# Decay weights of a recurrent layer: their tanh with tokens on the partitions, their running sums as matrix products

## The chip, the cores and the metric

The kernel runs on one core of a Trainium2 chip. The metric is device time in microseconds (us), the median of several runs. The engines are TensorE (PE; its weight loads are PEld), VectorE (DVE), ScalarE (ACT), GpSimd (POOL) and SyncE (SP), which here only issues transfers between SBUF and DRAM.

## The reference, cut to what matters

The program is a step through four layers: a long convolution (hyena), an attention layer, a recurrent layer (RWKV-7) and again hyena. Only the third, the recurrent one, is touched. It has D = 1024 channels in 16 heads of 64, T = 1152 tokens (1024 + 128), two directions n, and a state S for each head:

```python
r, k, v, z = einsum('pbld,pde->pble', [xr, xk, xv, xg], w_in)
wl = w0[n] + tanh(xw @ w1[n]) @ w2[n]                 # rank 64
decay = exp(-exp(-softplus(-wl) - 0.5))
a  = sigmoid(a0[n] + (xa @ a1[n]) @ a2[n])            # rank 64
kk = heads(k * k_k);  kk = kk * rsqrt(sum(kk * kk, -1) + 1e-12)
kd = heads(k * (1 + (a - 1) * k_a));  bd = kk * heads(a)
# at each token, forwards for n = 0 and backwards for n = 1:
S = S * decay + (S @ -kk) bd^T + v kd^T;   y = S @ r
```

Since exp(-softplus(-x)) is the sigmoid of x, the logarithm of a decay is -exp(-0.5) (1 + tanh(wl / 2)) / 2. The kernel takes the tokens in chunks of 64 and needs, in each chunk, the products of the decays up to every token, and their inverses. These are exponentials of running sums of 1 + tanh(wl / 2).

## The kernel before

Constants: P = 128 partitions, KC = 8 blocks of 128 channels (index b), NG = 3 groups of GRP = 384 tokens (index g), 6 chunks of 64 in a group. Activations lie with channels on the partitions and tokens along the row.

The recurrent layer (`rwkv`, line 1569) has three stages. First `dense` (line 1696) runs a list of jobs, each a projection of one block of 128 output channels: for each g it accumulates 8 x 3 fp32r matmuls of 384 columns (`mm3`, lines 262 to 264: high part times high part, and two products with low parts) in one PSUM bank, and an `evac` function takes the bank out. The order of jobs is r (8 jobs), `wjob` (the rank-64 hidden part of the decays, 3 steps for both directions), v (8), `ajob` (the same for a), k (8), z (8). The weights of the next job are loaded after a job's first step into tiles with tags `wh` and `wl`, two of each. The inputs of a job are mixed from the activations by `mix` (line 1648) into four slots, as far ahead as slots come free (`mix_ahead`); it works in tiles with tags `mix` and `nb`, two of each.

The second stage overlaps with the k and z jobs: `weave` (line 1888) takes in turns the 44 last steps of `dense` and the generators `rows_of(b)` (line 1802), three pieces for each g, 24 groups in all. A group loads r, v and k (`rvk`, line 1812, in a tile with tag `mix`), makes the decays' pre-activation from the hidden part with `lora2` (lines 1740 to 1745: one matmul with 128 rows and one with 64), takes tanh on ScalarE (L1822), adds 1 (L1824), forms the running sums of a chunk with a scan on VectorE, one for each direction (L1827; `rst` resets it every 65 columns), turns the second direction's sums round on GpSimd (L1846, L1847) and takes exponentials (L1840 to L1849). W holds the decay products and `ei` their inverses, all in SBUF. The norms of the keys are spread by transposes (L1832) into PSUM, and L1835 makes the normalised keys `kk` in SBUF. From these, a and k come the rows `ct` and `bk` (L1855 to L1865), which are stored for the third stage, and a bonus term (L1862 to L1871, with one plain fp32 matmul, L1869, that becomes two instructions). The third stage, the chunked recurrence, only reads what is stored.

PSUM has eight banks; `set_banks` (line 1874) lets tags mm, tp and ax take all eight in turn through the first two stages. Each bank is one tile, so a tile that takes a bank waits for its last reader. The instructions of an engine run in the order in which the planner put them at build time, which follows the order of the program except where it finds other work ready earlier; on the chip that order is fixed.

Of the kernel before, what the change touches and what calls it, by code (L numbers as in the profile page):

```python
# [132 lines left out]
def rwkv_constants():  # L133
    q = np.arange(64)
    blk = np.kron(np.eye(2), np.ones((64, 64)))
    eye = np.zeros((P, P))
    eye[:, :64] = np.concatenate([np.eye(64)] * 2)
    eye[:, 64:66] = np.kron(np.eye(2), np.ones((64, 1)))
    row, colm = q[:, None], q[None, :]
    mask = np.zeros((P, 2, P))  # L140
    for n, (st, inc) in enumerate(((row < colm, row <= colm), (row > colm, row >= colm))):
        mask[:, n, :64] = np.concatenate([st] * 2)
        mask[:, n, 64:] = np.concatenate([inc] * 2)
    lm = np.zeros((P, 4, 2, 64))
# [15 lines left out]
    reset = (np.arange(6 * 65) % 65 != 0).astype(np.float32)  # L160
    return (np.stack([blk, eye], 1).astype(np.float32), mask.astype(np.float32), four.astype(np.float32),
            levels.reshape(P, 4, 256).astype(np.float32), reset)


def weave(*jobs):

    for _ in woven(*jobs):
        pass
# [29 lines left out]
def chain_gens(*gens):  # L198
    for g in gens:
        yield from g  # L200
# [22 lines left out]
class Prog:  # L223
# [1345 lines left out]
    def rwkv(self, i, rest):  # L1569
# [20 lines left out]
        v_.tensor_scalar(hka[:, :, 1], vec[:, :, 5], -0.5, 1.0, op0=M, op1=Ad)  # L1590
        v_.tensor_scalar(hka[:, :, 2:], vec[:, :, :4], 0.5, None, op0=M)
        wcs = keep.tile([P, KC, 2 * NCH], F32, name="wcs")
        cdec = math.exp(-0.5)
        eps = keep.tile([P, 2], F32, name="eps")
        v_.memset(eps[:, 0:1], 1e-12)
# [100 lines left out]
        def dense(jobs):  # L1696

            nxt, later = self.load_w(jobs[0][0]), None  # L1700
            for n, (_, mi, evac) in enumerate(jobs):
                wh, wl = nxt
                for g in range(NG):
                    o = self.psum("mm")[:, :GRP]
                    hh, hl = slot(3 * mi + g)
                    for k in range(KC):
                        self.mm3(o, wh[:, k], wl[:, k], hh[:, k], hl[:, k], k == 0, k == KC - 1)
                    if later:
                        later()
                    later = evac(g, o)  # L1710
                    if g == 0 and n + 1 < len(jobs):
                        nxt = self.load_w(jobs[n + 1][0])
# [5 lines left out]

        def lora(mi, name, fn):

            hid = [pool.tile([P, T], F32R, name=f"{name}{n}") for n in range(2)]
# [24 lines left out]

        wjob, whid = lora(1, "w", AF.Tanh)
        ajob, ahid = lora(3, "a", AF.Copy)

        def project(p, mi, evac):  # L1750
            return [(A["rw_w_in"][p, :, b * P:(b + 1) * P], mi, lambda g, ps, b=b: evac(b, g, ps)) for b in range(KC)]
# [50 lines left out]
        def rows_of(b):  # L1802

            if b in (0, 1, 2, 4):
                bs = slice(b, b + max(b, 1))
                s_.activation(norms[:, bs], norms[:, bs], AF.Sqrt, bias=eps[:, 0:1])
                v_.reciprocal(norms[:, bs], norms[:, bs])
            w2 = [lora2_weights(name, b) for name in "wa"]
            for g in range(NG):
                gs = grp[g]  # L1810
                x = pool.tile([P, 3, GRP], F32, tag="mix", name="rvk", bufs=2)
                nc.sync.dma_start(x, rvk[b, :, :, gs])
                r, v, k = (x[:, y] for y in range(3))
# [4 lines left out]
                W = pool.tile([P, 2, 6, 65], F32, tag="nb", name="W", bufs=2)  # L1818
                v_.memset(W[:, :, :, 0], 0.0)
                c3 = lambda x: x.rearrange("p (c t) -> p c t", t=64)  # L1820
                for n in range(2):
                    s_.activation(W[:, n, :, 1:], c3(lora2(w2[0], whid, g, n)), AF.Tanh, scale=0.5,  # L1822
                                  bias=hka[:, b, 2 + n:3 + n])
# [4 lines left out]
                rx = self.mp.tile([P, 512], F32, tag="mprod", name="rx", bufs=1)[:, :GRP].rearrange("p (c t) -> p c t", t=64)  # L1828
                s_.copy(rx, norms[:, b, 6 * g:6 * g + 6].unsqueeze(2).broadcast_to([P, 6, 64]))
                pb = self.psum("tp")[:, :GRP]  # L1830
                for o in range(3):
                    nc.tensor.transpose(pb[:, o * P:(o + 1) * P], rx[:, 2 * o:2 * o + 2].rearrange("p a b -> p (a b)"),  # L1832
                                        self.ident)
                kk = row2()
                v_.scalar_tensor_tensor(kk, k, vec[:, b, 4:5], pb, op0=M, op1=M)  # L1835
                for n in range(2):
                    s_.activation(an[:, n], c3(lora2(w2[1], ahid, g, n)), AF.Tanh, scale=0.5,
                                  bias=hka[:, b, 4 + n:5 + n])
                yield
                s_.activation(wcs[:, b].rearrange("p (d c) -> p d c", d=2)[:, :, 6 * g:6 * g + 6], W[:, :, :, 64], AF.Exp,  # L1840
                              scale=-cdec / 2)
                ei = [self.mp.tile([P, 512], F32, tag=f"macc{n}", name="ei", bufs=1)[:, :6 * 65] for n in range(2)]
                ei = [x.rearrange("p (c t) -> p c t", t=65) for x in ei]
                s_.activation(ei[0], W[:, 0], AF.Exp, scale=cdec / 2)
                last = ei[1][:, :, 64:65]
                g_.tensor_copy(last, W[:, 1, :, 64:65])  # L1846
                g_.tensor_tensor(W[:, 1], last.broadcast_to([P, 6, 65]), W[:, 1], Su)  # L1847
                s_.activation(ei[1], W[:, 1], AF.Exp, scale=cdec / 2)
                s_.activation(W, W, AF.Exp, scale=-cdec / 2)  # L1849
# [3 lines left out]
                upto, before = (AP(W.tensor, W.offset + x, [W.ap[0], [390 + 1 - 2 * x, 2], [65, 6], [1, 64]]) for x in (1, 0))  # L1853
                ei = [ei[0][:, :, 1:], ei[1][:, :, :64]]
                g_.tensor_tensor(kd, kd, both(k), M)  # L1855
                v_.tensor_tensor(ct[:, :, :, 0], before, both(kk), M)
# [23 lines left out]
        weave((part_gen(run, 6 * KC + 6 - DS), 6 * KC + 6 - DS), (rest, 44))  # L1880
        mtmp.close()
        pool2 = tmp.enter_context(tc.tile_pool(name="rw2", bufs=1, side="right", reuse_waits="tile"))
        rst = pool2.tile([P, 6 * 65], F32, name="rst")
        nc.sync.dma_start(rst, A["rw_reset"].partition_broadcast(P))
# [395 lines left out]
def host_arrays(x):  # L2280
# [37 lines left out]
    r["rw_const"], r["rw_mask"], r["rw_lmask"], r["rw_levels"], r["rw_reset"] = rwkv_constants()  # L2318
    return r


# [17 lines left out]
```

## Time and profile before

| | us |
|---|---|
| median of three runs | 4572.27 (4570.69 to 4586.91) |
| the profiled execution's own time | 4590.18 |
| its span | 4588.4 |
| projections of r, v, from | 2030 to 2331 |
| `ajob` and first k steps | 2331 to 2382 |
| row groups beside k and z jobs | 2382 to 2791 |

Over the span TensorE is busy for 89%, VectorE for 76%, ScalarE for 52% and GpSimd for 51%. The stretch of the change is under a tenth of the span, so shares of the whole say little of it; the rows below are from that stretch. Busy time of TensorE counts the whole passage of a matmul, and neighbours overlap, so the distance between two starts, not the length of one, tells what a stream of matmuls costs.

### The profile page before, as it was taken

The page shows a single profiled execution, that of the slowest core. Times are in us where ns is not written, and L with a number is a line of the kernel's source. Part 1 is how long each engine was busy: PE and PEld are TensorE (multiplying, and loading weights), DVE is VectorE, ACT ScalarE, POOL GpSimd, SP SyncE. Part 2 cuts the span into 40 slices and gives each one's busy share as a digit, 9 for nine tenths or more (in the row PEclk, how much of TensorE's full clock was granted, in tenths as well). Part 3 has the DMA queues.
Part 4 walks back from the last instruction along what each step waited for, and adds up shares of the span by engine and source line. Part 5 has one row for each costly group of instructions (what it writes and reads, how often), then busy time and mean ns, then how long its engine had stood idle before and what let it go on. Part 6 is the DMA issues. An engine that isn't in the chain of part 4 may idle for free. (4 is left out here: it accounts for less than half of the span.)

```text
span 4588.4 us, 83899 instructions
## 1 busy us (share of the span) xinstructions
PE 4061.0 (89%) x30888; PEld 3510.6 (77%) x30888; DVE 3504.3 (76%) x6147; ACT 2392.5 (52%) x5468; POOL 2360.3 (51%) x1902
## 2 busy tenths in 40 slices
PE   7988988889999999879979786999999889988988
PEld 4888888678777776658867575878888678878986
DVE  7777888655998999687587997677767668967877
ACT  5554433455666666453455553666666456543331
POOL 3655766253677877455555564333333233466550
PEclk8999999999999999989988797999999899999999
DMA  5755555643000000326635464222322424665455
GB/s 169 239 181 176 164 156 157 191 149 99 19 22 21 18 28 30 121 91 203 188 108 198 145 222 136 59 79 84 83 75 68 142 93 120 214 205 153 141 155 179
DMA packets 490982, 583.04 MB, mean 127 GB/s; under 512 B 59818, under 2 KB 378332, under 8 KB 489932
## 3 DMA queue, kind: packets, MB, share of 16 engines
q1 hardware_dynamic: 489068, 576.70, 40.7%
q8 instruction: 244, 4.00, 0.4%
q14 instruction: 166, 1.36, 0.1%
q10 hardware_dynamic: 1504, 0.98, 0.1%
HBM read 413.74 MB, written 161.37 MB: 125 GB/s over the span
## 5 line engine op out<-in xcount | busy, mean ns | idle before, releaser
L262 PE MATMUL ps_mm<-hh,wh 128*128 128x384 f32 x1728 | 597.0, 347 | 47.4 <-ACT hh L267 24.0
L263 PE MATMUL ps_mm<-hl,wh 128*128 128x384 f32 x1728 | 595.6, 345 | 2.8 <-DVE hl L268 1.8
L264 PE MATMUL ps_mm<-hh,wl 128*128 128x384 f32 x1728 | 594.5, 344 | 2.7 <-POOL wl L268 2.7
L1499 POOL TENSOR_TENSOR sm<-sm,pf 128x512 f32<-128x512 f32 x288 | 443.4, 1540 | 121.8 <-ACT pf L1492 48.8
L268 POOL TENSOR_TENSOR wl<-wraw,wh 128x512 fp32r<-128x512 f32 x212 | 331.5, 1581 | 187.4 <-ACT wh L267 175.3
L262 PEld LDWEIGHTS ps_mm<-hh,wh 128*128 128x128 f32 x1728 | 335.9, 195 | 55.5 <-ACT hh L267 25.1
L1497 DVE TENSOR_TENSOR wl<-pf,wh 128x512 fp32r<-128x512 f32 x288 | 352.8, 1235 | 6.6 <-ACT wh L1493 5.8
L263 PEld LDWEIGHTS ps_mm<-hl,wh 128*128 128x128 f32 x1728 | 336.2, 195 | 7.5 <-DVE hl L268 4.4
L264 PEld LDWEIGHTS ps_mm<-hh,wl 128*128 128x128 f32 x1728 | 336.0, 194 | 6.4 <-POOL wl L268 3.8
L305 POOL TENSOR_TENSOR macc<-macc,mprod 128x512 f32<-128x512 f32 x140 | 211.8, 1513 | 178.0 <-ACT mprod L304 155.4
L263 PE MATMUL ps_mm<-mx,wh 128*128 128x384 f32 x680 | 253.6, 373 | 37.9 <-DVE mx L1669 36.9
L262 PE MATMUL ps_mm<-mx,wh 128*128 128x384 f32 x680 | 255.9, 378 | 19.9 <-ACT mx L1668 6.1
L262 PE MATMUL ps_mm<-woh,hh 128*128 128x512 f32 x576 | 233.8, 407 | 37.0 <-ACT hh L267 34.6
L2144 POOL TENSOR_TENSOR tot<-SV,wcs 64x128 f32<-64x128 f32 x288 | 115.6, 405 | 267.9 <-DVE SV L2172 245.2
L264 PE MATMUL ps_mm<-mx,wl 128*128 128x384 f32 x680 | 247.0, 364 | 3.1 <-POOL wl L268 3.1
L1492 ACT ACTIVATE pf<-ps_st 128x512 f32<-128x512 f32 x288 | 172.3, 598 | 144.9 <-POOL sm L1499 53.3
L264 PE MATMUL ps_mm<-woh,hl 128*128 128x512 f32 x576 | 234.1, 406 | 3.7 <-DVE hl L268 3.7
L302 DVE SCALAR_TENSOR_TENSOR macc<-modw,cond,macc 128x512 f32<-128x512 f32 x140 | 156.5, 1118 | 103.3 <-DMA modw<-mod_w 102.4
L1437 DVE TENSOR_REDUCE mx<-ps_pj 128x1 f32<-128x512 f32 (+2 forms) x400 | 220.4, 575 | 17.2 <-PE ps_pj L1436 16.4
L263 PE MATMUL ps_mm<-wol,hh 128*128 128x512 f32 x576 | 231.8, 402 | 0.0
L304 ACT ACTIVATE mprod<-modw,cond 128x512 f32<-128x512 f32 x140 | 101.3, 723 | 205.5 <-POOL macc L305 108.6
L1493 ACT ACTIVATE wh<-ps_st 128x512 fp32r<-128x512 f32 x336 | 194.3, 578 | 0.0
(560 smaller groups left out, 13149.2 us busy)
## 6 DMA issues: line engine op xcount, KB each, us to landing
cst<-cst SPq DMA_DIRECT2D x175, 384.0 KB
modw<-mod_w SPq DMA_DIRECT2D x160, 256.0 KB
wraw<-hy_w_in SPq DMA_DIRECT2D x128, 256.0 KB
kd<-kt SPq DMA_DIRECT2D x72, 384.0 KB
kt<-kd SPq DMA_DIRECT2D x72, 384.0 KB
cst<-cst SPq DMA_DIRECT2D x41, 512.0 KB
ctd<-ct SPq DMA_DIRECT2D x24, 768.0 KB
bkd<-bk SPq DMA_DIRECT2D x24, 768.0 KB
```

The source lines that it names most:

```text
L262: mm(ps, lh, rh, start=start, stop=False)
L263: mm(ps, lh, rl, start=False, stop=False)
L264: mm(ps, ll, rh, start=False, stop=stop)
L268: (lo_eng or self.nc.gpsimd).tensor_tensor(lo, src, hi, ALU.subtract)
L302: nc.vector.scalar_tensor_tensor(acc[0], w, s, acc[0], op0=ALU.mult, op1=ALU.add)
L305: nc.gpsimd.tensor_tensor(acc[1], acc[1], wp, ALU.add)
L1437: nc.vector.tensor_reduce(mx[:, t, j:j + 1], ps, AX.X, ALU.max)
L1492: nc.scalar.activation(pf, s, AF.Exp, scale=scale)
L1493: nc.scalar.activation(ph, s, AF.Exp, scale=scale)
L1497: nc.vector.tensor_tensor(pl, pf, ph, ALU.subtract)
L1499: nc.gpsimd.tensor_tensor(sm, sm, pf, ALU.add)
L2144: g_.tensor_tensor(tot[h], SV[e][h, jsl], wc[h].unsqueeze(2).broadcast_to([64, 2, 64]), M)
```

## The change

The tanh of the decays is taken before the row groups, with tokens on the partitions, in two new jobs between v and `ajob`. Each (one for a direction) makes, for every tile of 128 tokens, two blocks of 512 channels: three matmuls (hidden part times high part of w2, 64 rows of it times the low part, and a product with constant rows of ones that adds the bias w0), a tanh from PSUM, and a store of the 128 x 1024 tile to a DRAM array `thd`. In the row groups the running sums are matrix products of these tiles with triangular 0/1 matrices `tri` (a sum is over the tokens, which now are the contraction); the +1 of each token enters as a one-row product with a table of counts. The second direction's triangle sums backwards, so its turning round is gone. The two sums of a group stay in PSUM (three banks of their own); W is their exponential in SBUF, the inverse decays are written over the sums in PSUM, and `kk` stays in the bank of the transposes. The other tags share five banks from there on. The hidden part of the decays moves to a pool that is closed before the row groups.

```diff
+        ones_r = keep.tile([P, 2, P], F32R, name="ones_r")
...
+            load = lambda n: self.load_w(jobs[n][0]) if jobs[n][1] is not None else jobs[n][0]()
+            nxt, later = load(0), None
             for n, (_, mi, evac) in enumerate(jobs):
                 wh, wl = nxt
+                if mi is None:
+                    nxt = load(n + 1)
+                    if later:
+                        later = later()
+                    yield from evac(wh, wl)
+                    continue
...
+        def decays(n):
+            h = half[n]
+
+            def steps(wh, wl):
+                for t in range(NT):
+                    ts = slice(t * P, (t + 1) * P)
+                    x = pool.tile([P, 3, GRP], F32, tag="mix", name="th", bufs=2).rearrange("p a c -> p (a c)")[:, :D]
+                    for cs in (slice(0, 512), slice(512, D)):
+                        ps = self.psum("ax")
+                        nc.tensor.matmul(ps, whid[n][:, ts], wh[:, cs], start=True, stop=False)
+                        nc.tensor.matmul(ps, whid[n][h, ts], wl[h, cs], start=False, stop=False)
+                        nc.tensor.matmul(ps, ones_r[:, n], wl[:, cs], start=False, stop=True)
+                        s_.activation(x[:, cs], ps, AF.Tanh, scale=0.5)
+                    nc.sync.dma_start(thd[:, t, :, n].rearrange("b p c -> p b c"), x.rearrange("p (b c) -> p b c", c=P))
...
-        jobs = project(0, 0, evac_r) + [wjob] + project(2, 2, evac_v) + [ajob]
+        jobs = project(0, 0, evac_r) + [wjob] + project(2, 2, evac_v) + [decays(0), decays(1), ajob]
...
-            w2 = [lora2_weights(name, b) for name in "wa"]
+            w2 = lora2_weights("a", b)
             for g in range(NG):
                 gs = grp[g]
+                th = pool2.tile([P, 3, 2, P], F32, tag="th", name="th", bufs=2)
+                nc.sync.dma_start(th, thd[b, 3 * g:3 * g + 3].rearrange("o p n c -> p o n c"))
...
+                sums = [self.psum("w")[:, :6 * 65] for _ in range(2)]
+                for n, ps in enumerate(sums):
+                    for o in range(3):
+                        own = ps[:, o * 130:(o + 1) * 130]
+                        nc.tensor.matmul(own, ones_r[:1, 1], cnt[:, n], start=True,
+                                         stop=False)
+                        nc.tensor.matmul(own, th[:, o, n], tri[:, n], start=False, stop=True)
...
-                kk = row2()
-                v_.scalar_tensor_tensor(kk, k, vec[:, b, 4:5], pb, op0=M, op1=M)
+                v_.scalar_tensor_tensor(kk, k, vec[:, b, 4:5], kk, op0=M, op1=M)
...
-                v_.tensor_scalar(W[:, :, :, 1:], W[:, :, :, 1:], 1.0, None, op0=Ad)
-                for n in range(2):
-                    w1 = W[:, n].rearrange("p c t -> p (c t)")
-                    v_.tensor_tensor_scan(out=w1, data0=rst, data1=w1, initial=0.0, op0=M, op1=Ad)
...
+                W = pool.tile([P, 2, 6, 65], F32, tag="nb", name="W", bufs=2)
+                for n, ps in enumerate(sums):
+                    s_.activation(W[:, n].rearrange("p c t -> p (c t)"), ps, AF.Exp, scale=-cdec / 2)
+                    s_.activation(ps, ps, AF.Exp, scale=cdec / 2)
...
+        self.set_banks(mm_tp_ax=(0, 1, 2, 3, 4), w=(5, 6, 7))
         weave((run, 6 * KC - 4), (chain_gens(*(rows_of(b) for b in range(KC))), 9 * KC))
```

## Rows read from the trace of the kernel before

**Rows 1.** Busy time by stretch: engines with record counts, granted clock, DMA share.

```profile
core 0: us, PE busy (x) PEld busy (x) DVE busy (x) ACT busy (x) POOL busy (x), PEclk, DMA share, GB/s
2331.00:2382.00 51.00, 35.65 (x143) 30.10 (x142) 39.76 (x78) 31.40 (x57) 21.88 (x13) 0.73 0.22 62
...
2560.00:2660.00 100.00, 72.59 (x282) 56.99 (x280) 89.70 (x118) 53.34 (x102) 60.97 (x42) 0.78 0.49 164
2660.00:2760.00 100.00, 87.65 (x406) 73.26 (x405) 93.49 (x100) 53.24 (x108) 63.56 (x47) 0.93 0.64 213
...
2382.00:2791.00 409.00, 337.17 (x1500) 279.37 (x1502) 350.18 (x426) 216.13 (x413) 243.88 (x175) 0.83 0.56 187
```

**Rows 2.** TensorE in order of time (start, length in us) in the row groups.

```profile
2564.56 0.81 PEld L1785 LDWEIGHTS ps_tp<-rwc,po 128*128 128x128 f32 x6
...
2705.43 0.42 PE L1743 MATMUL ps_ax<-w,w 128*128 128x384 f32 x1
2705.78 0.43 PE L1744 MATMUL ps_ax<-w,w 64*128 64x384 f32 x1
2706.14 0.44 PE L1743 MATMUL ps_ax<-w,w 128*128 128x384 f32 x1
...
2724.40 0.49 PE L1832 MATMUL ps_tp<-ident,rx 128*128 128x128 f32 x3
...
2728.65 0.34 PE L262 MATMUL ps_mm<-mx,wh 128*128 128x384 f32 x1
...
2729.17 0.34 PE L262 MATMUL ps_mm<-mx,wh 128*128 128x384 f32 x1
...
2751.15 0.81 PE L1869 MATMUL ps_ax<-row,rwc 128*128 128x384 f32 x2
```

**Rows 3.** Busy time of L262 alone, then of L1743 alone, by stretch.

```profile
2660.00:2760.00 100.00, 39.12 (x104) 21.36 (x104) 0.93 0.64 213
2660.00:2760.00 100.00, 10.84 (x29) 5.10 (x29) 0.93 0.64 213
```

**Rows 4.** Groups by line, 2382 to 2791: busy us, mean ns | idle before.

```profile
L1827 DVE TENSOR_TENSOR_SCAN W<-rst,W 128x390 f32<-128x390 f32 x48 | 63.6, 1361 | 0.5
L1864 DVE SCALAR_TENSOR_TENSOR bk<-bk,ei 128x384 f32<-128x384 f32 x48 | 57.6, 1219 | 2.4 <-ACT ei L1848 1.5
L1865 DVE TENSOR_TENSOR bk<-bk,ei 128x384 f32<-128x384 f32 x48 | 40.5, 882 | 2.6 <-POOL row L1862 2.4
L1856 DVE TENSOR_TENSOR ct<-W,row 128x768 f32<-128x768 f32 x24 | 37.2, 1549 | 2.8 <-POOL w L268 2.3 <-ACT W L1849 0.4
L1860 DVE SCALAR_TENSOR_TENSOR bk<-bk,row 128x768 f32<-128x768 f32 x24 | 31.0, 1291 | 3.3 <-ACT bk L1850 3.0
L1822 ACT ACTIVATE W<-ps_ax,hka 128x384 f32<-128x384 f32 x48 | 26.1, 579 | 12.9 <-PE ps_ax L1744 8.9 <-DVE ct L1856 3.4 <-POOL ei L1846 0.4
L1847 POOL TENSOR_TENSOR W<-ei,W 128x390 f32<-128x390 f32 x24 | 25.8, 1074 | 1.3 <-ACT wcs L1840 0.2
L1824 DVE TENSOR_SCALAR W<-W 128x768 f32<-128x768 f32 x24 | 19.8, 826 | 13.4 <-ACT W L1822 13.2
```

**Rows 5.** One line's instructions: duration ns min/median/max, first and last start.

```profile
L1864 DVE SCALAR_TENSOR_TENSOR bk<-bk,ei x48: 527/1274/2202, 2391.5 to 2785.5; 128x384 f32<-128x384 f32 x48
L1835 DVE SCALAR_TENSOR_TENSOR row<-rvk,rvec,ps_tp x24: 593/605/616, 2382.9 to 2780.1; 128x384 f32<-128x384 f32 x24
L1870 DVE TENSOR_TENSOR row<-ps_ax,rvk x24: 526/550/558, 2406.1 to 2790.1; 128x384 f32<-128x384 f32 x24
```

**Rows 6.** The chain that ended last, 2367 to 2791: start us, us, what.

```profile
2768.22 2.41 DVE bk L1864 x2
...
2771.50 1.76 DVE W L1827 x2
...
2774.87 5.10 DMA rvk<-rvk
...
2790.73 3.81 DMA bvd<-row
```

**Rows 7.** Waits of TensorE, 2300 to 2384: us in total, times, longest.

```profile
PE ps_mm L263 <- DVE mx L1669: 11.3, 7, 2.8
```

**Rows 8.** Waits of TensorE, 2382 to 2791: us in total, times, longest.

```profile
PE ps_ax L1869 <- DVE row L1867: 22.8, 10, 6.5
```

More of the change, by code (lines that the diff above doesn't have):

```diff
@@ L159, in rwkv_constants @@
     four = np.stack([four, four * (1 - 2 * lm_eye)], 1)
-    reset = (np.arange(6 * 65) % 65 != 0).astype(np.float32)
+    t65, two = np.arange(65), np.arange(P)
+    tri = np.zeros((P, 2, 2, 65))
+    for c in range(2):
+        own, s = (two // 64 == c)[:, None], (two % 64)[:, None]
+        tri[:, 0, c] = own & (s < t65)
+        tri[:, 1, c] = own & (s >= t65)
+    counts = np.stack([np.tile(t65, 2), np.tile(64 - t65, 2)]).reshape(1, -1)
     return (np.stack([blk, eye], 1).astype(np.float32), mask.astype(np.float32), four.astype(np.float32),
-            levels.reshape(P, 4, 256).astype(np.float32), reset)
+            levels.reshape(P, 4, 256).astype(np.float32), tri.reshape(P, 2, 130).astype(np.float32),
+            counts.astype(np.float32))
 def weave(*jobs):
@@ L1592, in rwkv @@
         wcs = keep.tile([P, KC, 2 * NCH], F32, name="wcs")
+        thd = self.dp.tile([KC, NT, P, 2, P], F32, name="thd")
+        ones_r = keep.tile([P, 2, P], F32R, name="ones_r")
+        for n, h in enumerate(half):
+            s_.activation(ones_r[h, n], self.ones[h], AF.Copy, scale=0.0)
+            s_.copy(ones_r[half[1 - n], n], self.ones[half[1 - n]])
         cdec = math.exp(-0.5)
@@ L1696, in dense @@
         def dense(jobs):
-            nxt, later = self.load_w(jobs[0][0]), None
+            load = lambda n: self.load_w(jobs[n][0]) if jobs[n][1] is not None else jobs[n][0]()
+            nxt, later = load(0), None
             for n, (_, mi, evac) in enumerate(jobs):
                 wh, wl = nxt
+                if mi is None:
[4 more added lines that the diff above has]
+                    continue
                 for g in range(NG):
@@ L1711, in dense @@
                     if g == 0 and n + 1 < len(jobs):
-                        nxt = self.load_w(jobs[n + 1][0])
+                        nxt = load(n + 1)
                     if n + 1 == len(jobs) or jobs[n + 1][1] != mi:
@@ L1719, in lora @@
         def lora(mi, name, fn):
-            hid = [pool.tile([P, T], F32R, name=f"{name}{n}") for n in range(2)]
+            hid = [(mpool if name == "w" else pool).tile([P, T], F32R, name=f"{name}{n}") for n in range(2)]
             def evac(g, ps):
@@ L1748, in rwkv, with decay_weights @@
         ajob, ahid = lora(3, "a", AF.Copy)
+        def decay_weights(n):
+            h, o = half[n], half[1 - n]
+            wh, wl = (self.wp.tile([P, KC, P], F32R, tag=x, name=x).rearrange("p k c -> p (k c)") for x in ("wh", "wl"))
+            for cs in (slice(0, 512), slice(512, D)):
+                raw, rows = (self.wp.tile([P, 4, P], F32, tag="wraw", name=x).rearrange("p k c -> p (k c)")
+                             for x in ("w2r", "w2b"))
+                for x in half:
+                    nc.sync.dma_start(raw[x], A["rw_w2"][h, cs])
+                s_.copy(wh[:, cs], raw)
+                g_.tensor_tensor(wl[h, cs], raw[h], wh[h, cs], Su)
+                v_.memset(rows[o], 0.0)
+                for x in (o.start, o.start + 32):
+                    nc.sync.dma_start(rows[x:x + 1], A["rw_wb"][n:n + 1, cs])
+                s_.copy(wl[o, cs], rows[o])
+                x = slice(o.start + 32, o.stop)
+                v_.tensor_tensor(wl[x, cs], rows[x], wl[x, cs], Su)
+            return wh, wl
+        def decays(n):
[4 more added lines that the diff above has]
+                    x = pool.tile([P, 3, GRP], F32, tag="mix", name="th", bufs=2).rearrange("p a c -> p (a c)")[:, :D]
+                    for cs in (slice(0, 512), slice(512, D)):
+                        ps = self.psum("ax")
[4 more added lines that the diff above has]
+                    nc.sync.dma_start(thd[:, t, :, n].rearrange("b p c -> p b c"), x.rearrange("p (b c) -> p b c", c=P))
+                    if t % 3 == 2:
+                        yield
+            return lambda: decay_weights(n), None, steps
         def project(p, mi, evac):
@@ L1815, in rows_of @@
                 an, kd = bk[:, :, :, 0], bk[:, :, :, 1]
-                W = pool.tile([P, 2, 6, 65], F32, tag="nb", name="W", bufs=2)
-                v_.memset(W[:, :, :, 0], 0.0)
+                sums = [self.psum("w")[:, :6 * 65] for _ in range(2)]
[5 more added lines that the diff above has]
+                        nc.tensor.matmul(own, th[:, o, n], tri[:, n], start=False, stop=True)
@@ new lines, in rows_of @@
+                rx = self.mp.tile([P, 512], F32, tag="mprod", name="rx", bufs=1)[:, :GRP].rearrange("p (c t) -> p c t", t=64)
+                s_.copy(rx, norms[:, b, 6 * g:6 * g + 6].unsqueeze(2).broadcast_to([P, 6, 64]))
+                kk = self.psum("tp")[:, :GRP]
+                for o in range(3):
+                    nc.tensor.transpose(kk[:, o * P:(o + 1) * P], rx[:, 2 * o:2 * o + 2].rearrange("p a b -> p (a b)"),
+                                        self.ident)
+                v_.scalar_tensor_tensor(kk, k, vec[:, b, 4:5], kk, op0=M, op1=M)
@@ L1828, in rows_of @@
[L1828 to L1833, printed above, removed]
-                kk = row2()
@@ L1835, in rows_of @@
-                v_.scalar_tensor_tensor(kk, k, vec[:, b, 4:5], pb, op0=M, op1=M)
-                for n in range(2):
-                    s_.activation(an[:, n], c3(lora2(w2[1], ahid, g, n)), AF.Tanh, scale=0.5,
-                                  bias=hka[:, b, 4 + n:5 + n])
-                yield
-                s_.activation(wcs[:, b].rearrange("p (d c) -> p d c", d=2)[:, :, 6 * g:6 * g + 6], W[:, :, :, 64], AF.Exp,
-                              scale=-cdec / 2)
-                ei = [self.mp.tile([P, 512], F32, tag=f"macc{n}", name="ei", bufs=1)[:, :6 * 65] for n in range(2)]
@@ L1843, in rows_of @@
[L1843 to L1849, printed above, removed]
+                    s_.activation(an[:, n], c3(lora2(w2, ahid, g, n)), AF.Tanh, scale=0.5, bias=hka[:, b, 4 + n:5 + n])
@@ new lines, in rows_of @@
+                yield
+                W = pool.tile([P, 2, 6, 65], F32, tag="nb", name="W", bufs=2)
+                for n, ps in enumerate(sums):
+                    s_.activation(W[:, n].rearrange("p c t -> p (c t)"), ps, AF.Exp, scale=-cdec / 2)
+                    s_.activation(ps, ps, AF.Exp, scale=cdec / 2)
+                s_.copy(wcs[:, b].rearrange("p (d c) -> p d c", d=2)[:, :, 6 * g:6 * g + 6],
+                        AP(W.tensor, W.offset + 64, [W.ap[0], [390 - 64, 2], [65, 6]]))
@@ L1853, in rows_of @@
                 upto, before = (AP(W.tensor, W.offset + x, [W.ap[0], [390 + 1 - 2 * x, 2], [65, 6], [1, 64]]) for x in (1, 0))
+                ei = [x.rearrange("p (c t) -> p c t", t=65) for x in sums]
                 ei = [ei[0][:, :, 1:], ei[1][:, :, :64]]
@@ L1879, in rwkv @@
         mix_ahead(-1)
-        weave((part_gen(run, 6 * KC + 6 - DS), 6 * KC + 6 - DS), (rest, 44))
+        weave((part_gen(run, 6 * KC + 12 - DS), 6 * KC + 12 - DS), (rest, 44))
         mtmp.close()
         pool2 = tmp.enter_context(tc.tile_pool(name="rw2", bufs=1, side="right", reuse_waits="tile"))
-        rst = pool2.tile([P, 6 * 65], F32, name="rst")
-        nc.sync.dma_start(rst, A["rw_reset"].partition_broadcast(P))
+        tri = pool2.tile([P, 2, 130], F32, name="tri")
+        nc.sync.dma_start(tri, A["rw_tri"])
+        cnt = pool2.tile([1, 2, 130], F32R, name="cnt")
+        raw = self.mp.tile([P, 512], F32, tag="macc0", name="cnr", bufs=1)[:1, :260]
+        nc.sync.dma_start(raw, A["rw_counts"])
+        s_.copy(cnt.rearrange("p n c -> p (n c)"), raw)
         row2 = lambda: self.mp.tile([P, 512], F32, tag="modw", name="row", bufs=2)[:, :GRP]
@@ L2317, in host_arrays @@
     r["state"] = f(x["state_rwkv"][0, 0].transpose(0, 1, 3, 2))
-    r["rw_const"], r["rw_mask"], r["rw_lmask"], r["rw_levels"], r["rw_reset"] = rwkv_constants()
+    r["rw_const"], r["rw_mask"], r["rw_lmask"], r["rw_levels"], r["rw_tri"], r["rw_counts"] = rwkv_constants()
+    r["rw_wb"] = f(x["rw_w0"][0])
     return r
```

2 lines of the change are left out of this document (removed).

## The prediction

> **What bounds the kernel now.** I first looked for the stage that holds the edited lines, with the view of busy time by stretch of time [rows 1]. The stage in which the row groups are made (line 1802) runs from 2382 to 2791 us, 409 us with 24 groups, so 17.0 us a group. VectorE is busy for 350.2 us of it, TensorE for 337.2, and the granted TensorE clock averages 0.83. Read alone, this says that VectorE ends last. But a busy TensorE isn't yet a TensorE at its peak, so I counted what it has to issue. When it streams, matmuls of 384 columns start 0.17 us apart [rows 2]: three steps from 2728.65 to 2729.17, so 0.173 each. A step of `dense` is 8 x 3 = 24 of them, 4.15 us. The product of `lora2` is a pair, one matmul with 128 rows and one with 64: alternating, they start 0.35 and 0.36 us apart [rows 2], so a change between 128 and 64 rows costs about 0.19 us beside the 0.173, and a pair takes 0.73. L1869 is 0.81 for its two, the three transposes of L1832 0.49, six matmuls of L1785 0.81 (from the weight loads).
>
> The stage's issue time is then 44 steps x 4.15 = 183; 24 groups x 4 pairs x 0.73 = 70; 24 x 0.81 = 19; 24 x 0.49 = 12; 22 x 0.81 = 18; together 302 us, 74% of 409. By stretch it is less even. From 2660 to 2760 there are 104 records of each dense line and 29 of L1743 [rows 3]: 3 x 104 x 0.173 = 54, 29 x 0.73 = 21, and 6 groups of L1869 and L1832 at 1.3 = 8, so 83 of 100 us at a granted clock of 0.93. TensorE has little room there. From 2560 to 2660, where the last input mixes also load VectorE, TensorE records fall to 282 and the clock to 0.78 [rows 1]: there VectorE really ends last. So a change that moves work from VectorE to TensorE meets two limits that lie close together.
>
> **Part 1: what leaves VectorE.** Gone are the scans L1827 (48 x 1.361 = 63.6 us) and the +1 of L1824 (24 x 0.826 = 19.8) [rows 4], 83 us. A second saving is less visible. L1864, all of whose tensors lie in SBUF, takes 527 ns at least but 1274 at the median and 2202 at most, while L1835 and L1870, which read one operand from PSUM, stay within 593 to 616 and 526 to 558 [rows 5]. GpSimd works beside all three. With inverse decays and keys in PSUM, L1864 should fall from 1219 to about 605, L1865 from 882 to 550, L1856 and L1860 from 1549 and 1291 [rows 4] to about 1000 (an estimate: their 768 elements against L1870's 384, twice 0.55 less one start): 48 x 0.61 + 48 x 0.33 + 24 x 0.55 + 24 x 0.29 = 29 + 16 + 13 + 7 = 65 us. VectorE goes from 350 to about 202 us, half of the stage. If it gained nothing from PSUM it would still be 267, 65%, so it no longer ends last by itself. GpSimd loses L1847 (25.8 us) and the small copy before it, and ScalarE's tanh of L1822 moves to an earlier stage. Both engines were idle for 40% or more [rows 1], so I cost that at nothing.
>
> **Part 2: what comes to TensorE in the same stage.** The decays' `lora2` pairs go: 48 x 0.73 = 35 us. In their place each group gets 6 sums of 130 columns: one one-row product that adds the counts (`cnt`), and one plain fp32 product `th` x `tri`, which like L1869 becomes two instructions. No row of this stage shows a one-row matmul between 128-row ones. The nearest is the 128/64 alternation, 0.19 a change, and a sum has two changes. The weights of plain fp32 matmuls follow each other in 0.81 / 6 = 0.135 us [rows 2], more than 130 columns need (2 x 130 / 384 x 0.173 = 0.12). So a sum costs 2 x 0.19 + 0.07 + 0.27 = 0.72 us, and 144 of them 104 us. If the change of rows were free: 0.34 each, 49 us. If each change cost 0.25, as under a stall, 0.84, 121 us. I take 104, since the alternation is the same kind of step in the same stage.
>
> A rule bears on exactly this gap. The Trainium skill (TensorEngine Tiling (Array Packing), Key Properties) says that changing the tiling mode, not only the tile, drains the engine. No run here shows it for one row; by it the sum is the 104 us, and without it 49.
>
> So TensorE's issue time goes from 302 to 302 - 35 + 104 = 371 us. With VectorE out of the way I let it fill 0.88 of the stage: more than the 0.83 of its best stretch here, less than 1, because the groups still hand work around four engines. 371 / 0.88 = 422 us, 13 us more than now. Bounds: free changes give (302 - 35 + 49) / 0.88 = 359 (50 less); a fill of only 0.83 gives 447 (38 more). At the end of the stage the last group's chain loses its two scans (1.76) and about half of the 2.41 us of its L1864 [rows 6]: 3 us less.
>
> **Part 3: the new job in the projection stage.** `decays` makes 36 blocks of 512 columns, three matmuls each. By columns one is 512 / 384 x 0.173 = 0.23; the middle one uses 64 rows, so two changes: 3 x 0.23 + 2 x 0.19 = 1.07, 39 us in all. But each 128-token tile (two blocks, 2.1 us) is stored to DRAM, 512 KB, from a tile with tag `mix`, of which there are two. A store of 192 KB takes 3.81 us to land and a load of 576 KB takes 5.10 [rows 6]. I take 4.5, and 1.2 us for two tanh (L1822 takes 0.58 for 384 columns [rows 4]). Two tiles in flight then give (1.2 + 4.5) / 2 = 2.85 us a tile, 18 x 2.85 = 51 us. ScalarE needs 21 us of that and VectorE nearly nothing. The weights of `decays` are loaded under the last v job. What is queued behind: the job after it, `ajob`, needs a weight tile with tag `wh`, and both are held by the two `decays` jobs, so `ajob` can start only when the first is done.
>
> Some of it is covered. From 2331 to 2382 TensorE shows 143 records, about 25 us of work in 51 us at a clock of 0.73 [rows 1], and it waits 11.3 us for VectorE's mixes in the stretch from 2300 on [rows 7]. The mixes of the first rows of `ajob` and k can run under `decays`; those behind `ajob` can't, because their slots come free only as `ajob` consumes them, and they use the same `mix` tiles. I take 5 us of waits covered and 6 us of `ajob` fitted into TensorE's gaps in the second half: 51 - 11 = 40 us. Bounds: 15 (39 us of issue less all 24 to 26 us that TensorE loses in that stretch) and 65 (the stores slow each other to 3.6 us a tile).
>
> **Part 4: the rest.** The new load `th` (384 KB a group) is issued on SP's queue beside `rvk`'s, into two tiles; both go out after the last bv store of an earlier group, and the DMA share is 0.56 [rows 1]. I cost it at nothing, covered by the group in flight; uncovered it is up to 24 x 0.5. The two removed `w2` loads and splits per b are off the path. The stage's PSUM goes from eight banks in one ring to a ring of five and three for the sums; `kk` now holds one of the five from its transposes until L1860. I cost this at nothing because `dense` fills a bank for 4.15 us and L1860 needs little before it; uncovered see rival 3.
>
> **The sum:** +13 - 3 + 40 = +50 us. The profiled execution is 4590.18 us, 18 above the median of the three runs, 4572.27; the same stage lengths are assumed for both. So 4590 becomes 4640 in a profile, and the median 4572 becomes 4622.
>
> **The rivals.** (1) The one-row product is nearly free of the change. Then the row stage is 50 us shorter, 3 us go at the tail, and `decays` costs 25 to 40: -28 to -13, about 4552, faster or the same. It decides from a price of about 0.35 us a sum; at 0.55 (316 + 144 x 0.21 = 346, / 0.88 = 393) rows gain 16 and the case is lost again. For it: no row prices a one-row matmul. Against: the 0.19 at every change of L1743 and L1744 [rows 2]. (2) VectorE was the real bound, and with it at half load TensorE fills 0.95 of the stage: 371 / 0.95 = 391, 18 less; with 3 at the tail and `decays` 40, +19, 4591. For it: the hole from 2560 to 2660, and TensorE's 22.8 us of waits for L1867 [rows 8]. (3) `kk`'s bank makes the next dense step wait for L1860 about 2 us in each of 24 groups: 48 more, 4670. For it: the ring returns to that bank after four tiles. Against: L1860 will come sooner on a lighter VectorE. That the change does not relieve VectorE at all (reads from PSUM stretched as well) I hold for unlikely, by L1835 and L1870 [rows 5].
>
> **How the numbers follow.** Forecast case 0.45 (4595 to 4650 by its own bounds), rival 1 0.20, rival 2 0.20, rival 3 0.15. Half a per cent, 23 us, is about what a measurement of this kernel tells from no change. The forecast case gives slower 0.41 and same 0.04; rival 1 faster 0.12 and same 0.08; rival 2 same 0.13, slower 0.05, faster 0.02; rival 3 slower 0.15. So faster 0.14, same 0.25, slower 0.61. The range reaches to the faster half of rival 1, 4548, and to rival 3's time, 4670, and leaves out a tenth on either side.
>
> **What would show it.** In the changed profile: VectorE's total in the row stage near 200 us with L1864 near 0.6; TensorE starts of the one-row products 0.2 us or more behind their neighbours; the row stage near 420 us; between the last v job and `ajob` some 40 us with TensorE waiting for stores of `th`. The forecast is wrong if the one-row matmuls stream without gaps, if `decays` runs at 2.1 us a tile beside mixes that stalled anyway, or if TensorE's clock and fill in the row stage rise well above 0.93 and 0.88.

## The result and the profile after

The changed kernel takes 1.0141 (1.0117 to 1.0165) of the time before, 4648 against 4580 us. A second set of runs, beside 13 of the kernel before, gave 4639.79 against 4588.75, 1.0112 (1.0077 to 1.0146): slower by 69 and by 51 us, where 50 was forecast. The profiled execution of the first set was disturbed (its granted clock was 0.684), so the rows below are those of the second set; its own time was 4646.61, its span 4644.8.

First the ends of the stretches: starts of the first and last instruction of three lines of the kernel after. L1817 stores r, L1893 makes the keys of a row group, L1925 is the last product of a group.

```profile
L1817 SPq DMA_DIRECT2D rvk<-po x24: 319/360/462, 2018.8 to 2141.3; - x24
L1893 DVE SCALAR_TENSOR_TENSOR ps_tp<-rvk,rvec,ps_tp x24: 608/622/623, 2425.5 to 2822.2; 128x384 f32<-128x384 f32 x24
L1925 DVE TENSOR_TENSOR row<-ps_ax,rvk x24: 548/558/559, 2440.9 to 2840.9; 128x384 f32<-128x384 f32 x24
```

From before, r's first store; the other two are L1835 and L1870 of [rows 5].

```profile
L1756 SPq DMA_DIRECT2D rvk<-po x24: 319/366/594, 2030.2 to 2153.4; - x24
```

So two lengths describe each kernel: **projections**, from the first store of r to the first keys of a row group, and **rows**, from there to the last start of L1925. Before they are 2382.9 - 2030.2 = 352.7 and 2790.1 - 2382.9 = 407.2; after, 406.7 and 415.4: +54 and +8. The work ahead of r's first store is the same in both kernels and ended between 2014 and 2035 us in the executions shown here, and what lies behind the rows takes 1785 to 1804 us in them (1798 before, 1804 after), so some ten us of any span are not the change's doing.

The rows' stretch after, busy time by stretch, answers to [rows 1].

```profile
core 0: us, PE busy (x) PEld busy (x) DVE busy (x) ACT busy (x) POOL busy (x), PEclk, DMA share, GB/s
2425.00:2841.00 416.00, 384.19 (x1801) 319.28 (x1800) 194.94 (x331) 185.11 (x372) 166.48 (x117) 0.86 0.60 200
```

VectorE fell from 350 to 195 us and the stretch is no shorter. Where the relief went: TensorE in order of time, five of the sums, to be read as the distances of the starts of L1884.

```profile
2636.74 0.32 PE L1884 MATMUL ps_w<-cnt,ones_r 1*128 1x130 f32 x1
2636.99 0.49 PE L1886 MATMUL ps_w<-tri,th 128*128 128x130 f32 x2
2637.41 0.33 PE L1884 MATMUL ps_w<-cnt,ones_r 1*128 1x130 f32 x1
2637.67 0.49 PE L1886 MATMUL ps_w<-tri,th 128*128 128x130 f32 x2
2638.09 0.32 PE L1884 MATMUL ps_w<-cnt,ones_r 1*128 1x130 f32 x1
...
2638.76 0.32 PE L1884 MATMUL ps_w<-cnt,ones_r 1*128 1x130 f32 x1
...
2639.44 0.32 PE L1884 MATMUL ps_w<-cnt,ones_r 1*128 1x130 f32 x1
```

A sum takes 0.675 us, at a granted clock of 1.00. VectorE's four lines that now read PSUM (by line, 2425 to 2841) answer to L1864, L1865, L1856 and L1860 of [rows 4]:

```profile
L1919 DVE SCALAR_TENSOR_TENSOR bk<-bk,ps_w 128x384 f32<-128x384 f32 x48 | 24.8, 549 | 0.4
L1920 DVE TENSOR_TENSOR bk<-bk,ps_w 128x384 f32<-128x384 f32 x48 | 24.8, 549 | 10.9 <-POOL row L1917 10.7
L1911 DVE TENSOR_TENSOR ct<-W,ps_tp 128x768 f32<-128x768 f32 x24 | 22.9, 953 | 37.9 <-ACT W L1900 35.1 <-issue 2.5
L1915 DVE SCALAR_TENSOR_TENSOR bk<-bk,ps_tp 128x768 f32<-128x768 f32 x24 | 22.8, 951 | 22.5 <-ACT bk L1904 22.5
```

Of the longest waits of TensorE in this stretch, which answer to [rows 8], VectorE's share has shrunk: L1924 (before L1869) waits 5.9 us once, and the dense step waits for L1915, the last reader of `kk`'s bank, twice. The longest is one for ScalarE.

```profile
PE ps_tp L1891 <- ACT rx L1888: 9.2, 1, 9.2
PE ps_mm L270 <- DVE bk L1915: 7.9, 2, 5.4
PE ps_ax L1924 <- DVE row L1922: 5.9, 1, 5.9
```

Now the decays jobs. TensorE in order of time; the distance of two starts of L1801 is one block of 512 columns.

```profile
2291.35 0.48 PE L1801 MATMUL ps_ax<-wh,w 128*128 128x512 f32 x1
...
2292.53 0.40 PE L1801 MATMUL ps_ax<-wh,w 128*128 128x512 f32 x1
...
2295.30 2.34 PE L322 MATMUL ps_ax<-ones,macc 128*128 128x1 f32 x16
...
2299.57 0.78 PE L1801 MATMUL ps_ax<-wh,w 128*128 128x512 f32 x1
...
2301.59 0.63 PE L1801 MATMUL ps_ax<-wh,w 128*128 128x512 f32 x1
...
2304.74 0.79 PE L1803 MATMUL ps_ax<-wl,ones_r 128*128 128x512 f32 x1
2315.09 0.80 PE L1801 MATMUL ps_ax<-wh,w 128*128 128x512 f32 x1 [9.55 <-ACT th L1804]
...
2331.56 0.63 PE L1801 MATMUL ps_ax<-wh,w 128*128 128x512 f32 x1
2332.12 0.79 PE L1802 MATMUL ps_ax<-wl,w 64*128 64x512 f32 x1
2332.84 0.79 PE L1803 MATMUL ps_ax<-wl,ones_r 128*128 128x512 f32 x1
2333.44 0.63 PE L1801 MATMUL ps_ax<-wh,w 128*128 128x512 f32 x1
```

A block takes 1.18 us at first and 1.88 us later. Busy time by stretch shows the granted clock beside it:

```profile
2290.00:2300.00 10.00, 8.51 (x38) 5.76 (x38) 8.85 (x11) 6.63 (x13) 4.83 (x3) 0.83 0.71 196
2300.00:2310.00 10.00, 5.54 (x9) 2.14 (x8) 9.88 (x17) 4.67 (x8) 6.29 (x5) 0.50 0.34 83
2310.00:2320.00 10.00, 4.12 (x6) 1.65 (x6) 9.86 (x15) 6.01 (x10) 6.09 (x4) 0.50 0.44 142
...
2344.00:2354.00 10.00, 10.00 (x17) 4.21 (x16) 0.00 (x0) 5.27 (x10) 0.00 (x0) 0.50 0.75 228
...
2374.00:2384.00 10.00, 10.00 (x56) 10.00 (x55) 3.86 (x7) 6.58 (x14) 1.46 (x1) 0.94 0.88 262
```

TensorE fills its first eight banks until 2305, then waits 9.55 us for the first tanh, which stands on ScalarE's queue behind the input mixes of `ajob`; these go at VectorE's pace (9.9 of 10 us busy). The granted clock falls to 0.50, the lower level of 1.2 GHz, before that wait and not in it: the block that starts at 2299.57 already takes 2.02 us. Ahead of the fall stand five blocks and the sixteen one-column products of L322. The clock stays low to 2374, through the wait and then 50 us in which TensorE shows hardly a gap. From 2315 on, 28 blocks are left: 28 x 1.88 = 53 us, which ends at 2368; the last L1803 starts at 2369.1.

### The profile page after: what moved, and what is told of

Read it like the earlier page. It is cut to its first block, busy times and chain, and to the rows that moved or that the text cites. A ratio compares the mean times of both kernels' runs of the same rounds, so it can differ in the third digit from the quotient of the medians.

```text
span 6603.6 us, 84719 instructions
## 1 busy us (share of the span) xinstructions
PE 6426.6 (97%) x31332; PEld 4864.4 (74%) x31332; DVE 3202.6 (48%) x6059; ACT 2419.6 (37%) x5485; POOL 2131.0 (32%) x1850
## 5 line engine op out<-in xcount | busy, mean ns | idle before, releaser
L270 PE MATMUL ps_mm<-hh,wh 128*128 128x384 f32 x1728 | 903.7, 524 | 30.4 <-ACT hh L275 21.8
L272 PE MATMUL ps_mm<-hh,wl 128*128 128x384 f32 x1728 | 906.7, 525 | 0.0
L271 PE MATMUL ps_mm<-hl,wh 128*128 128x384 f32 x1728 | 906.2, 525 | 0.0
L270 PEld LDWEIGHTS ps_mm<-hh,wh 128*128 128x128 f32 x1728 | 468.3, 271 | 131.7 <-issue 38.4
L271 PEld LDWEIGHTS ps_mm<-hl,wh 128*128 128x128 f32 x1728 | 465.9, 270 | 91.1 <-issue 30.0
L272 PEld LDWEIGHTS ps_mm<-hh,wl 128*128 128x128 f32 x1728 | 461.3, 267 | 95.2 <-issue 35.3
L270 PE MATMUL ps_mm<-woh,hh 128*128 128x512 f32 x576 | 348.5, 606 | 17.3 <-ACT hh L275 17.3
L271 PE MATMUL ps_mm<-wol,hh 128*128 128x512 f32 x576 | 346.9, 602 | 0.0
L270 PE MATMUL ps_mm<-mx,wh 128*128 128x384 f32 x680 | 334.4, 494 | 10.6 <-DVE bk L1915 5.8
L271 PE MATMUL ps_mm<-mx,wh 128*128 128x384 f32 x680 | 332.3, 490 | 12.8 <-DVE mx L1684 12.8
L275 ACT CAST wh<-wraw 128x512 fp32r<-128x512 f32 x212 | 122.0, 618 | 403.4 <-PE ps_mm L271 332.5
```

Source lines behind the costliest of these rows:

```text
L270: mm(ps, lh, rh, start=start, stop=False)
L271: mm(ps, lh, rl, start=False, stop=False)
L272: mm(ps, ll, rh, start=False, stop=stop)
L275: self.nc.scalar.copy(hi, src)
```

## The experiments

Each ratio is to the kernel before, run beside that kernel. Kernels that were not run beside each other are compared by their ratios.

**The changed kernel again, and the decays jobs alone.**

> The changed kernel, unaltered, for a profile to be laid beside that of the kernel before: 1.014 of before. By the forecast the row stage (from the first group to the last bonus) takes 419 us instead of 409 and the stretch between the last v job and ajob is 40 us longer. By the rival of kk's bank the row stage takes about 465 us and TensorE waits for L1915's bank; by the rival in which VectorE was the bound it takes under 395 us and the decays jobs cost nearly 80.

4639.79 us, as told above. The second kernel is the one before with the jobs put in:

```diff
-        jobs = ... project(2, 2, evac_v) + [ajob]
+        jobs = ... project(2, 2, evac_v) + [decays(0), decays(1), ajob]
```

> The kernel before with the two decays jobs put in between v and ajob and their tiles stored, but not read: the row groups are those of before. By the forecast 40 us more than before (15 to 65), so about 4620. If the whole difference of the change lies in the decays jobs, 65 to 70 more; if it lies in the row stage, under 20.

4635.14 us, 1.0105 (1.0074 to 1.0136), 46 over before with 14 us of uncertainty; its projections take 405.5 us, 53 more than before. So the jobs alone cost about what the whole change costs, and all edits of the row groups together come to 4639.79 - 4635.14 = 5 us, which is within the noise. The rows of the traces say the same: 411.5 us here, 415.4 in the changed kernel.

**Whether the changes of rows eat VectorE's relief.** In the changed kernel the counts are padded with zero rows, so that their product has 128 rows like its neighbours:

```diff
-        nc.tensor.matmul(own, ones_r[:1, 1], cnt[:, n], start=True,
+        nc.tensor.matmul(own, ones_r[:, 1], cnt[:, n], start=True,
```

> The changed kernel with the counts' product over 128 rows (all but the first are zero) instead of one row: the same number of instructions, the same columns, but no change of rows on TensorE in the sums. By the forecast's price of two changes of 0.19 us in each of 144 sums the row stage loses 55 us of TensorE's issue time, and the run is 40 to 60 us faster than the changed kernel, about 4595. If one-row products are free of the change, within 8 us of the changed kernel.

4593.66 us, 1.0014 (0.9997 to 1.003), 46 under the changed kernel. TensorE in order of time, three sums:

```profile
2642.68 0.31 PE L1884 MATMUL ps_w<-cnt,ones_r 128*128 128x130 f32 x1
2642.82 0.44 PE L1886 MATMUL ps_w<-tri,th 128*128 128x130 f32 x2
2643.01 0.31 PE L1884 MATMUL ps_w<-cnt,ones_r 128*128 128x130 f32 x1
2643.16 0.43 PE L1886 MATMUL ps_w<-tri,th 128*128 128x130 f32 x2
2643.35 0.31 PE L1884 MATMUL ps_w<-cnt,ones_r 128*128 128x130 f32 x1
```

0.335 us a sum. As many matmuls, as many columns, 128 times the rows, half the time: 144 x (0.675 - 0.335) = 49 us of issue, and the rows' stretch is 367.9 us, 47.5 shorter. Both changes of rows are seen: the start behind a one-row product comes 0.11 us later than behind the padded one (0.25 against 0.14), and the start of the next one-row product 0.23 us later (0.42 against 0.19).

**Whether VectorE bounded the rows before.** The kernel before without L1824 and L1827.

> The kernel before without the +1 and the scans (L1824, L1827), which leaves the running sums out of the computation: only VectorE's relief of 83 us, with nothing added for TensorE. If VectorE ends last in the row stage, 40 to 66 us faster than before (TensorE's 302 us at a fill of 0.88 would be 343 of 409); if TensorE's own order and its changes of rows hold the stage, under 15 us faster.

4543.37 us, 0.9909 (0.9878 to 0.994), 45 under before; rows 372.4 us, 35 shorter. Of 83 us taken from VectorE 35 came out in the rows of the trace and 45 in the medians. So the relief was real, and worth about as much as the one-row products cost.

**What bounds the decays jobs.** The kernel before with both jobs, and the store of `th` taken out:

```diff
-                    nc.sync.dma_start(thd[:, t, :, n]..., x...)
```

> The kernel before with the two decays jobs put in, but their tiles are not stored to DRAM (that part is left out; nothing in this kernel reads them). Theory A, from the trace of the changed kernel: the jobs are bound by TensorE, which runs at a granted clock of 0.50 through them, so that the blocks start 1.88 us apart (36 x 1.88 = 68 us); without the stores it stays as with them, 35 to 58 us over before. Theory B, the prediction's own: the stores through two tiles set the 2.85 us a tile (51 us); without them the jobs take TensorE's issue time of the prediction, 39 us, and the kernel ends 12 us or more earlier than with stores, 20 to 34 us over before.

4642.23 us, 1.0106 (1.0085 to 1.0128), the same as with stores. Its blocks stand 1.88 us apart too, and its granted clock is 0.50 (TensorE in order of time, then busy time by stretch):

```profile
2344.87 0.63 PE L1791 MATMUL ps_ax<-wh,w 128*128 128x512 f32 x1
...
2346.75 0.63 PE L1791 MATMUL ps_ax<-wh,w 128*128 128x512 f32 x1
```

```profile
2346.00:2356.00 10.00, 10.00 (x17) 4.41 (x17) 0.55 (x1) 4.52 (x8) 3.73 (x3) 0.50 0.26 77
```

So it isn't the stores that bound the jobs. They may hold what follows: in the traces the projections are 396.8 us here against 405.5 with stores, and the last tanh comes as much sooner. The medians show nothing of these 9 us.

Then the changed kernel with decays' second and third product in one, of 128 rows (`ho` holds the hidden rows and the ones side by side):

```diff
-    nc.tensor.matmul(ps, whid[n][h, ts], wl[h, cs], start=False, stop=False)
-    nc.tensor.matmul(ps, ones_r[:, n], wl[:, cs], start=False, stop=True)
+    nc.tensor.matmul(ps, ho[:, t % 3], wl[:, cs], start=False, stop=True)
```

> The changed kernel with the decays' second and third product merged into one over 128 rows (the 64 rows of hidden values and the 64 rows of ones side by side in one stationary tile, made by two copies for each three token tiles). No matmul of 64 rows is left in the job and 72 matmuls stand where 108 stood. Theory A (TensorE at 1.2 GHz bounds the job): a block takes 0.92 to 1.2 us instead of 1.88, 33 to 43 us for all; the stores of the prediction (2.85 us a tile, 51 us) come next, so the kernel ends 13 to 28 us before the changed kernel. Theory B (the stores bound it already): 0 to 5 us.

4640.98 us, 1.011 (1.0093 to 1.0126): by the median no gain, with about 18 us of uncertainty on the difference. The trace has the gain where it was expected, at its lower edge: projections 393.9 us, 13 less. TensorE in order of time:

```profile
2335.06 0.63 PE L1806 MATMUL ps_ax<-wl,ho 128*128 128x512 f32 x1
2335.49 0.63 PE L1805 MATMUL ps_ax<-wh,w 128*128 128x512 f32 x1
2335.92 0.63 PE L1806 MATMUL ps_ax<-wl,ho 128*128 128x512 f32 x1
2338.11 0.50 PE L1805 MATMUL ps_ax<-wh,w 128*128 128x512 f32 x1 [1.57 <-ACT th L1807]
```

ScalarE's tanh of this kernel (duration ns min/median/max, first and last start):

```profile
L1807 ACT ACTIVATE th<-ps_ax x36: 588/595/616, 2324.4 to 2373.9; 128x512 f32<-128x512 f32 x36
```

Its longest wait, 2310 to 2375 (us in total, times, longest):

```profile
ACT th L1807 <- DMA thd<-th: 14.4, 13, 2.7
```

A block now takes 0.86 us at the lower level, and TensorE waits for tanh, tanh for stores. The 17 steps from the first tile to the eighteenth, 2324.4 to 2373.9, are 2.91 us each (in the changed kernel L1804 runs from 2314.4 to 2378.2, 3.75 a tile). That is near the 2.85 of the prediction, a bound that only shows once TensorE's is gone.

**The same, measured where it can be told.** Without the counts (Sigmoid in decays, both Exp with twice the scale), with three products and with two:

```diff
-                        s_.activation(x[:, cs], ps, AF.Tanh, scale=0.5)
+                        s_.activation(x[:, cs], ps, AF.Sigmoid)
...
-                        nc.tensor.matmul(own, ones_r[:1, 1], cnt[:, n], start=True,
-                                         stop=False)
```

> The changed kernel without the counts' products (Sigmoid in decays, both Exp with twice the scale), and with decays' three products left as they are: against the kernel with two products and no counts (0.9965 of before) this shows what the merged product is worth. Theory A (TensorE at 1.2 GHz bounds decays with three products; the traces show 13 us less from the first store of r to the first row group with two): 10 to 16 us more than with two products, 0.9985 to 1.000 of before. Rival (what the merged product wins in the stage is given back behind it): 0.9955 to 0.9975 of before.

> As the kernel with two products in decays, and the one-row products of the counts are gone: decays applies Sigmoid instead of Tanh, and both Exp take twice the scale, so that nothing has to be added to the sums. Theory A (the change of rows is what the one-row products cost): the 46 us that 128-row counts gave, and 144 x 0.07 / 0.88 = 11 us more for the products themselves, beside the 13 to 28 us in decays: 70 to 85 us under the changed kernel, 25 to 40 us under before. Rival: without its changes of rows the row stage is bound by other engines or loads (th and rvk, 960 KB a group), and the 11 us don't show: 59 to 74 us under the changed kernel.

> The kernel with two products and without counts once more, to stand on the same chip beside the one with the mixes woven in: ratio to before 0.994 to 0.998, as the first time.

Three products: 4585.5 us, 1.001 (0.9994 to 1.0027). Two: 4569.39 us, 0.996 (0.9942 to 0.9977), and again 4568.81, 0.9965 (0.9949 to 0.9981). The merged product is worth 0.45 to 0.5%, some 20 us with about 11 of uncertainty; the projections of the traces (403.6 and 394.4 us) show 9 of them, and where the rest lies is not shown. Rows are 356.0 and 355.4 us, 12 under those with 128-row counts, as expected; the median with three products shows of this only 2 us, within its interval. The kernel with two products and no counts is the fastest here: some 70 us under the changed kernel, where both theories met, and 15 to 20 under before, where 25 to 40 were expected.

**Whether `kk`'s bank holds up the dense steps.** The changed kernel with `kk` in SBUF:

```diff
-                v_.scalar_tensor_tensor(kk, k, vec[:, b, 4:5], kk, op0=M, op1=M)
+                kk = row2()
+                v_.scalar_tensor_tensor(kk, k, vec[:, b, 4:5], pb, op0=M, op1=M)
```

> The changed kernel with kk (the normalised keys) written to an SBUF tile, so that the bank of its transposes comes free at once. Theory A: kk's bank costs little (TensorE waited 7.9 us for L1915 before its dense steps in the whole row stage), and VectorE has room: time within 8 us of the changed kernel, while the two operations on kk that read SBUF again take 1.2 to 1.6 us instead of 0.95. Rival 3 of the prediction: the bank makes dense steps wait, up to 2 us a group; the kernel gets 10 to 48 us shorter.

4645.14 us, 1.0118 (1.0096 to 1.014): no difference. VectorE's two lines in the rows' stretch:

```profile
L1912 DVE TENSOR_TENSOR ct<-W,row 128x768 f32<-128x768 f32 x24 | 31.6, 1319 | 20.8 <-ACT W L1901 20.6
L1916 DVE SCALAR_TENSOR_TENSOR bk<-bk,row 128x768 f32<-128x768 f32 x24 | 30.7, 1280 | 48.3 <-ACT bk L1905 47.7 <-issue 0.4
```

The same operations took 953 and 951 ns from PSUM. That is over a quarter less, and it is worth nothing here, since VectorE no longer ends last. GpSimd, which works beside them, shows the same: its two products on `ct` and `bk` took 2153 and 2352 ns in the mean with the keys in SBUF, against 1675 and 1846 in the changed kernel (L1912 and L1910 there).

**Whether the tanh behind the mixes costs its 10 us.** The steps of `ajob`'s mixes are issued one behind each tile of decays, in the changed kernel and in the one with two products and no counts. In both kernels three of the twelve steps (part of the last group's mix) are left out.

```diff
+                    next(ahead, None)        # one step of a mix, behind each tile
```

> The changed kernel with one difference: the input mixes of ajob (3 groups, 12 steps) are no longer issued in one go ahead of decays, but one step behind each token tile of decays, so that the first tanh of decays doesn't stand behind them on ScalarE's queue. In the trace of the changed kernel TensorE waits 9.55 us for that tanh (2305.5 to 2315.1), and its granted clock falls to 0.50 in that stretch and stays there. Theory A (queue order on ScalarE): the wait goes, 8 to 15 us under the changed kernel with the clock still at 0.50 (1.88 us a block), and 25 to 40 under it if the clock stays up (1.18 us a block). Rival: the mixes have to be made in the same stretch and share the two tiles with tag mix with the stores, so what is won at the start is lost again: 0 to 5 us, or slower.

> The kernel with two products in decays and without the counts, and the mixes of ajob woven into decays as above. The jobs are then bound by the stores (2.75 us a tile in the kernel with two products, 18 tiles = 50 us) and the 10 us of wait ahead of the first tanh goes. Theory A: 10 to 20 us under the kernel with two products and no counts, some 30 to 40 us under before. Rival (mixes and stores share two tiles): 0 to 5 us under it, 20 to 25 under before.

4632.54 us, 1.0102 (1.0083 to 1.0121), and 4577.83, 0.9985 (0.9971 to 0.9999), against 0.9965 without weaving beside it. The first is some 5 us under the changed kernel, which is within the noise and where the rival had it. The second is 9 us slower than without weaving, a loss that neither theory had, although both woven kernels make three mix steps fewer. In the first of the two, TensorE's waits for tanh (2290 to 2385; us in total, times, longest) come to more than the one long wait of 9.55:

```profile
PE ps_ax L1811 <- ACT th L1814: 15.8, 6, 4.7
```

In the second kernel these waits are 38.2 us, against 22.3 without weaving. And in the first the clock falls all the same, though TensorE is busy throughout the 10 us in which it falls (busy time by stretch):

```profile
2300.00:2310.00 10.00, 10.00 (x40) 5.80 (x39) 1.88 (x5) 3.19 (x6) 0.12 (x1) 0.82 0.52 118
2310.00:2320.00 10.00, 4.61 (x7) 1.64 (x6) 4.53 (x8) 4.32 (x7) 2.28 (x2) 0.50 0.87 256
```

## Why the prediction was right, and where it was not

**The sum** was +50; the pair measured together gave +51, the first set +69. That the two agree within 1 us is partly luck: in the traces the two parts are +8 and +54, 62 together, and the larger part came out near its forecast through two errors that cancel (below).

**VectorE's relief** (Part 1): 202 us forecast, 195 measured; 0.61, 0.55 and about 1.0 us forecast for the four lines, 0.549, 0.549 and 0.95 measured. That reading PSUM is what makes L1911 and L1915 short is shown by the keys in SBUF, which bring them to 1.32 and 1.28 (1.55 and 1.29 before); for the other two no run shows it alone.

**The row stage** (Part 2): +13, with 3 off at the tail, was forecast; +8 in the traces, +5 in the medians. A sum was put at 0.72 and took 0.675, so TensorE's issue is 302 - 35 + 144 x 0.675 = 364 us, 0.88 of 415.4: the fill taken in the prediction. Free of the changes a sum was put at 0.34 and took 0.335. So rival 1 had its condition wrong and its price of a sum right. With 128-row counts the rows are 39 us shorter than before, where it had 50, the decays jobs take that back, and the case comes out beside before. The Trainium skill (TensorEngine Tiling (Array Packing), Key Properties) says that a change of tiling mode drains the engine; the traces agree for one row between 128-row neighbours, 0.675 against 0.335 us. They show the price and not the drain itself.

**Rival 2** had a true premise: VectorE bounded the rows before, as the kernel without the scan shows (35 us in its rows, 45 in the medians). But a lighter VectorE didn't lift TensorE's fill to 0.95. It stayed at 0.88, and is 315 / 367.9 = 0.86 with 128-row counts. **Rival 3** was wrong: L1915 comes soon enough, with two waits in the stage, and freeing its bank changed nothing.

**The decays jobs** (Part 3): +40 forecast, +46 measured (+54 in the traces), but for another reason. The step that failed is the limit: (1.2 + 4.5) / 2 = 2.85 us a tile through two `mix` tiles. Its sign, TensorE waiting for the stores of `th`, did not come: behind the first tanh TensorE waits hardly at all, and without stores its blocks stand as far apart. The issue time of 1.07 us a block was near at the full clock (1.18) and far off at the lower level (1.88), so that TensorE needs 3.75 us a tile and hides the stores. The prediction had the 0.73 of [rows 1] before it as the clock of that stretch, and priced TensorE at the full clock all the same. The jobs occupy TensorE from 2288 to 2369, 81 us, and cost 46 to 54, so 27 to 35 us of them were covered. The first eight blocks stand beside the end of v and in the stretch where the kernel before stalls for mixes too [rows 7]; that this is the cover is read from the order of the trace, and no run tests it. Forecast were 51 us less 11: the jobs were put some 30 us too short and their cover some 20 too small, and the two errors nearly cancel. The cover of 5 us for the mixes was misjudged too: the mixes don't only run under decays, they hold back its first tanh.

What stays open is why the clock fell and what it would have needed to rise again. The long wait was not the cause: the clock fell ahead of it, and with the wait cut up it fell too. No kernel here ran the jobs at the upper level throughout.

## What to carry to other kernels

A small correction product costs by its shape, not only by its columns: here padding a one-row matmul between full ones to 128 rows halved the sum, and folding it into a constant took it away. Price matmuls at the clock that the stage's own rows show. Work put between two stages sits behind what the engines' queues already hold, so look for its first instruction there. When a forecast comes out, check its parts: here two terms were off by some 20 and 30 us, in opposite directions.

## What the runs showed of the hardware that was not expected

A granted clock of 0.50 held for some 50 us while TensorE was busy for 9.7 to 10 of every 10 us, with 16 to 18 matmuls of 512 columns in each; it was at 0.94 in the slice of `ajob`'s dense steps (56 matmuls). In the woven kernel it fell in a slice of 10 us in which TensorE was busy for all 10. At the lower level a sum with a one-row product took 1.13 us (starts of L1884 at 2605.33 and 2606.46 in the changed kernel) against 0.675. VectorE's operations of 768 elements on two SBUF tensors and GpSimd's beside them each got shorter, by 26 to 28% and by 22%, when one of VectorE's tensors was in PSUM.
